# Two layers of a hybrid backbone with experts: outputs of six pairs by way of DRAM, inputs of layer 1 by gathers, shorter lists

## The chip, the cores and the metric

The kernel runs on one core of a Trainium2 chip (trn2). The metric is device time in microseconds (us); three runs of a kernel stand behind a median, and a trace of one profiled execution stands beside them.

## The reference

Two layers work on 256 latent and 256 context tokens of 1024 features, in float32. Each layer has a mixer (linear attention and grouped-query attention in layer 0, a state-space scan and a Fourier mix in layer 1) and then a mixture of 16 experts, of which each token uses two:

```python
idx, gates = route(tokens, router_w, router_b)      # two experts of one group of four
y = moe_ffn(tokens, idx, gates, exp_w_gate[layer], exp_w_up[layer], exp_w_down[layer])
x = layer_norm(alpha * x + m_lat[5] * y[n_ctx:].reshape(bsz, seq, d), ln_g[layer, 1], ln_b[layer, 1])
# an expert: (silu(xb @ w_gate) * (xb @ w_up)) @ w_down, hidden width 768
```

Layer 0 sends all 512 tokens through its experts, the last layer the 256 latent ones alone. The output is the latent stream.

## The kernel before

An expert's weights are six loads of 1.5 MB: four of gate and up (`in_egu`), two of down (`in_ed`). SyncE's queue (SP) issues them in order into slots (`wload`, L329); a load waits until PE has used what lay in its slot. Layer 0 has ten slots, layer 1 twelve.

The experts (`experts`, L1448) go two at a time, a pair. `route` gives every token its position in the lists of its two experts. `lists` (L1474) turns positions into a one-hot matrix G and, by a product with a table `aux` of four columns per token, into the slots' token numbers and gates. A list is cut into parts of 32 slots; S is the half (slots 0 to 63 or 64 to 127) of which a part is.

In layer 0 the tokens' rows lie in DRAM (`store`, L1431), and GpSimd (POOL) gathers those of a half list into the tile `xg` by an indirect DMA (`gather`, L1522); eight transposes per half bring features to the partitions (`features`, L1533, product `xt`). In layer 1 the rows stay in SBUF and the transposes are products with the one-hot matrix, two per block of features:

```python
for j in range(nb):
    self.mm(p[k // 4][:, (k % 4) * 128:(k % 4 + 1) * 128], xg[j][:, k * 128:(k + 1) * 128], G[S][:, j],
```

`hidden` (L1588) makes gate and up of each part (product `gu`), `down` (L1630) the outputs (product `dp`) of the expert before, whose results ACT and DVE take out of PSUM as a high and a low part `y`. `combine` (L1564) adds a pair's outputs to the tokens: DVE makes eight one-hot matrices, and PE multiplies them with `y`, 16 products of 512 columns in layer 0 (256 in layer 1) for the first half and 16 more where a list of the pair has over 64 slots (product `cm`); DVE adds the sums to `acc` (L1562). It comes one pair late, after gate and up of the second expert of the next pair.

Parts that a list doesn't reach are skipped by a branch (`when`, L1456): PE then runs a product with zeros in their place, so that PSUM holds zeros. In layer 0 the first two parts always run, in layer 1 the first. Lists over 128 slots would go through a loop of further windows at the end; the inputs have none. In layer 0 the fuller lists of the eight pairs have 74, 37, 62, 109, 101, 54, 67 and 61 slots, in layer 1 40, 39, 35, 68, 39, 38, 19 and 38 (worked out from the inputs with the reference's routing).

While the experts run, the order of PE's instructions is that of the program (`keep_in_program_order`); the other engines are ordered by a scheduler, and each engine works its list in order.

Of the kernel before, what the change touches and what calls it, by code (L numbers as in the profile page):

```python
# [8 lines left out]
F32 = mybir.dt.float32  # L9
# [23 lines left out]
NONE = 1024.0  # L33
R1, R2, R3 = 3, 4, (3, 5)
# weight slots in the areas while the experts run
# [3 lines left out]
# ---------------------------------------------------------------- host layout  # L39
# [13 lines left out]
# parameters and constants: '' for the whole run, 'A' and 'B' for the mixers of the two layers  # L53
# [79 lines left out]
def host_layout(a):  # L133
# [41 lines left out]
    # (layer, third, k, half, p, 1024): sixteen units per third, in loads of three and one  # L175
# [19 lines left out]
    # (l, e, k quarter, p, k, tile, gate or up, feature): each tile holds a quarter of the features  # L195
# [3 lines left out]
    # (l, e, half, p, b, output): the partitions hold the b-th 32 features of each quarter  # L199
# [56 lines left out]
# generators, each a step at a time  # L256
# [6 lines left out]
# pieces of one tile  # L263
# [11 lines left out]
class Core:  # L275
# [26 lines left out]
    # the four 16 KB areas b, o, a, x hold whatever lives across the parts of a layer  # L302
# [11 lines left out]
    # activations: a table set asked for is loaded behind those that need the one before, and before those that need it  # L314
# [62 lines left out]
    # between the layers: LayerNorm, and the modulated input of layer 1  # L377
# [29 lines left out]
    # out = x * exp(-ln(1 + exp(-x))); t is scratch  # L407
# [6 lines left out]
    # a third of layer l's adaLN rows for both streams, as per-partition scalars mods[l][:, m, kt, stream]  # L414
# [28 lines left out]

    def layer0(self):
# [27 lines left out]
    # acc = alpha * x + m2 * (o @ w_o); LayerNorm; v = modulated x for the experts; acc = alpha * x  # L472
# [31 lines left out]
    # layer 1's acc = alpha * x + m2 * (o @ w_o), over the features A of o, there before the others, and then B;  # L504
    # of the first N outputs all of A first
# [71 lines left out]
    # out = modulated, and x = alpha * (affine) of the normalized x, the stream h of acc  # L577
# [17 lines left out]
    # rows 0, 1: scale and offset of modulate(n * g + b); rows 2, 3: those of alpha * (n * g + b)  # L595
# [11 lines left out]
    # x (128, KT, n) <- (x - mean) / sqrt(var + eps) over the features, in place  # L607
# [32 lines left out]
    # a stream's LayerNorm, in parts of n tokens, each followed by what is done with it  # L640
# [18 lines left out]
    # scratch of normalize  # L659
# [9 lines left out]
    # x (in place) and its two parts, exact in float32r, of the modulated input  # L669
# [15 lines left out]
    # a weight chunk in two parts  # L685
# [8 lines left out]
    # x in two parts, exact in float32r  # L694
# [9 lines left out]
    # a product of two operands in parts: all but that of the two low parts, which is below float32's accuracy  # L704
# [7 lines left out]
    def even_mixer(self, uT, u, W):  # L712
# [6 lines left out]
        # low-rank decay inputs: partial sums over k on four column tiles  # L719
# [41 lines left out]
        # scratch: the places of the gated linear attention's later results, and the input's  # L761
# [35 lines left out]
    def attention(self, oT, gk, gv):  # L797
        nc, pt = self.nc, self.pt
        # the keys in two parts: the high one of each kv head on both halves of the partitions, the low one where the keys are
        kh = [pt.tile([128, T], F32R, name=f'kh{c}') for c in range(2)]  # L800
        kl = pt.tile([128, T], F32R, name='kl')
        for c in range(2):
            r = slice(c * 64, c * 64 + 64)
            for z in range(2):
                self.act(kh[c][z * 64:z * 64 + 64], gk[r], AF.Copy)
            nc.vector.tensor_tensor(kl[r], gk[r], kh[c][r].bitcast(F32), op=OP.subtract)
        for strm in range(2):
# [44 lines left out]
    def gla_states(self, i, q, k_, v, dec, mem):  # L852
# [3 lines left out]
        for di in range(2):  # L856
# [17 lines left out]
            # att[(cp, m), pair, l] = sum_d ke[d, m] qe[d, l], then its causal half  # L874
# [35 lines left out]
    def gla_heads(self, i, S, v, oT, mem):  # L910
        nc = self.nc
        for hh in range(2):
# [14 lines left out]
            # RMS norm over the value features  # L927
# [20 lines left out]
    # heads i (partitions 0-63, kv 0) and i + 4 (partitions 64-127, kv 1)  # L948
    def attend(self, q, k, v, oT, i, strm):
# [4 lines left out]
        # a head's queries in two parts, the high one where they are, the low one on the other half of the partitions  # L954
# [41 lines left out]
    # ------------------------------------------------------------ layer 1 mixer  # L996
# [21 lines left out]
    def odd_mixer(self, uT, parts):  # L1018
# [3 lines left out]
        # by streams: of the context's, nothing is needed once the states are there  # L1022
# [7 lines left out]
        # dt rows: heads of direction 0 at partitions 0-11, of direction 1 at 32-43  # L1030
# [19 lines left out]
        with tc.tile_pool(name='mixB1', bufs=1) as p1:  # L1050
# [17 lines left out]
            # token-major x and b, where the input was  # L1068
# [26 lines left out]
    def dt_tables(self, lr):  # L1095
# [28 lines left out]
        # weights of the tokens in their chunk's final state: dt * exp(sum of the later log decays)  # L1124
# [12 lines left out]
        # decay over the first latent chunk of each direction, on every partition  # L1137
# [38 lines left out]
    def ssd_heads(self, xb, xt, cs, HS, tabs, zs, oT, middle, last):  # L1176
# [4 lines left out]
        # the decays in two parts, exact in float32r, and what picks the rows of both  # L1181
# [266 lines left out]
    def experts(self, l, nb, pm, rows, xg, zero, pos, number, aux):  # L1448
# [25 lines left out]
        def lists(nm, n, e0, pos, aux, then=None):  # L1474
# [16 lines left out]
            if l:  # L1491
                if then:
                    then(Gs)
# [273 lines left out]
```

## Time and profile before

| | |
|---|---|
| median of three runs | 1545.85 us (1538.41 to 1550.7) |
| profiled execution, span from first to last instruction | 1528.9 us |
| PE busy | 1298.6 us, 85% |
| VectorE (DVE) busy | 755.5 us, 49% |
| mean DMA rate | 260 GB/s, 397.60 MB |

The profiled execution gives its span; the times of the runs also hold what lies around it, 16.95 us at the median. Layer 0's experts lie between about 389 and 860 us, layer 1's between about 1098 and 1507 us.

### The profile page before, as it was taken

What the parts mean: (1) busy time and instruction counts of PE and PEld (TensorE: products, weight loads), DVE (VectorE), ACT (ScalarE), POOL (GpSimd) and SP (SyncE); (2) the same over time, 40 slices, a digit from 0 to 9 for tenths busy, and PEclk for the clock granted to TensorE, in tenths of its full rate; (3) what the DMA queues carried; (4) which work ended last, traced back from release to release, by engine and by line L of the source; (5) the groups of instructions that cost most, each with busy time, mean ns of one, the idle gap of its engine ahead of it and who ended that gap; (6) DMA issues with size and microseconds to landing.
All of it is one profiled execution on the core that took longest, in us unless ns stands there. A gap on an engine that the chain in (4) does not pass through costs nothing. (4 is left out here: it accounts for less than half of the span.)

```text
span 1528.9 us, 28267 instructions
## 1 busy us (share of the span) xinstructions
PE 1298.6 (85%) x11753; PEld 799.5 (52%) x11754; DVE 755.5 (49%) x1899; ACT 417.4 (27%) x831; POOL 66.1 (4%) x68
## 2 busy tenths in 40 slices
PE   3999987996889889999988779989696778987774
PEld 0787643684334454665445348858442455544433
DVE  2756447776426233233344487567541544344534
ACT  3533243452112111111111243444321211121213
POOL 0000002011000000000000030030100000000000
PEclk8999988998899999999999989999898999999876
DMA  9322666044678978779987222652788998999931
GB/s 388 121 93 83 247 249 262 0 172 173 271 304 339 398 300 332 321 293 383 387 359 293 111 85 83 223 204 100 313 321 342 378 373 354 387 375 416 410 129 30
DMA packets 43700, 397.60 MB, mean 260 GB/s; under 512 B 4976, under 2 KB 9200, under 8 KB 12272
## 3 DMA queue, kind: packets, MB, share of 16 engines
q1 hardware_dynamic: 41200, 388.40, 63.1%
q0 software_dynamic: 1728, 4.20, 0.8%
q8 instruction: 158, 2.59, 0.7%
q10 hardware_dynamic: 576, 2.10, 0.3%
q14 instruction: 38, 0.31, 0.1%
HBM read 393.63 MB, written 3.15 MB: 260 GB/s over the span
## 5 line engine op out<-in xcount | busy, mean ns | idle before, releaser
L1599 DVE SCALAR_TENSOR_TENSOR h0p<-gu0p,gt0p,sg0p 128x192 f32<-128x192 f32 x64 | 25.1, 414 | 156.3 <-ACT sg0p L316 155.8
L1599 DVE SCALAR_TENSOR_TENSOR h1p<-gu1p,gt1p,sg1p 128x192 f32<-128x192 f32 x64 | 26.5, 414 | 142.2 <-ACT sg1p L316 142.2
L340 PE MATMUL gu1p<-more,big 128*32 128x384 f32 x976 | 87.2, 497 | 8.9 <-issue 5.1
L340 PE MATMUL gu0p<-big,xe0p 128*32 128x384 f32 x992 | 92.5, 494 | 0.2 <-DVE h0p L1599 0.2
L316 ACT ACTIVATE sg0p<-gu0p 128x192 f32<-128x192 f32 x64 | 19.7, 332 | 215.0 <-PE gu0p L340 211.8
L316 ACT ACTIVATE y0p<-dp0p 64x512 fp32r<-64x512 f32 x64 | 37.9, 591 | 147.9 <-PE dp0p L340 105.0
L340 PE MATMUL gu0p<-ring,xe0p 128*32 128x384 f32 x768 | 75.1, 490 | 1.5 <-ACT sg0p L316 0.8
L340 PE MATMUL gu0p<-more,xe0p 128*32 128x384 f32 x800 | 73.7, 488 | 0.9 <-issue 0.9
L1655 DVE TENSOR_TENSOR y0p<-dp0p,y0p 64x512 fp32r<-64x512 f32 x64 | 44.0, 688 | 58.2 <-ACT y0p L316 57.6
L340 PE MATMUL ada<-ring,small 128*32 128x512 f32 x344 | 60.1, 641 | 14.4 <-DMA ring<-in_ada 14.4
L316 ACT ACTIVATE sg1p<-gu1p 128x192 f32<-128x192 f32 x64 | 21.2, 330 | 183.5 <-PE gu1p L340 159.9
L340 PE MATMUL dp0p<-big,hT0p 128*32 128x256 f32 x792 | 59.6, 390 | 8.7 <-issue 6.1
L340 PEld LDWEIGHTS gu1p<-more,big 128*32 128x32 f32 x976 | 39.5, 112 | 51.6 <-issue 37.8
L1655 DVE TENSOR_TENSOR y1p<-dp1p,y1p 64x512 fp32r<-64x512 f32 x64 | 44.0, 688 | 42.9 <-ACT y1p L316 40.2
L340 PEld LDWEIGHTS gu0p<-big,xe0p 128*32 128x32 f32 x992 | 47.9, 111 | 32.9 <-issue 20.3
L316 ACT ACTIVATE y1p<-dp1p 64x512 fp32r<-64x512 f32 x64 | 37.8, 591 | 93.0 <-PE dp1p L340 49.1
L1562 DVE SCALAR_TENSOR_TENSOR big<-cm0p,mods,big 128x256 f32<-128x256 f32 x128 | 51.6, 476 | 20.0 <-PEq L1460 10.0
L340 PE MATMUL gu1p<-big 128*32 128x384 f32 x528 | 54.5, 521 | 4.0 <-issue 4.0
L340 PE MATMUL cm0p<-oh0p,y0p 128*128 128x512 f32 x192 | 55.2, 417 | 2.7 <-DVE big L1562 1.2
L316 ACT ACTIVATE big<-big 128x512 f32<-128x512 f32 (+2 forms) x81 | 44.7, 575 | 46.7 <-DVE big L626 19.4
L340 PE MATMUL zo<-zo,zw 128*128 128x256 f32 x384 | 54.6, 292 | 0.0
L340 PEld LDWEIGHTS zo<-zo,zw 128*128 128x128 f32 x384 | 48.6, 191 | 6.6 <-issue 4.3
(537 smaller groups left out, 2483.8 us busy)
## 6 DMA issues: line engine op xcount, KB each, us to landing
more<-in_egu SPq DMA_DIRECT2D x54, 1536.0 KB, 11.1
big<-in_egu SPq DMA_DIRECT2D x48, 1536.0 KB, 13.9
ring<-in_ada SPq DMA_DIRECT2D x27, 1536.0 KB, 7.3
ring<-in_ed SPq DMA_DIRECT2D x27, 1536.0 KB, 9.4
ring<-in_egu SPq DMA_DIRECT2D x26, 1536.0 KB, 10.1
big<-in_ed SPq DMA_DIRECT2D x21, 1536.0 KB, 10.6
more<-in_ed SPq DMA_DIRECT2D x16, 1536.0 KB, 10.6
ring<-in_odw SPq DMA_DIRECT2D x5, 1536.0 KB, 7.5
```

Of the source, the lines that this page charges most:

```text
L316: a = self.nc.scalar.activation(out, x, func, **kw)
L340: i = self.nc.tensor.matmul(out, lhsT, rhs, start=start, stop=stop, skip_group_check=True)
L1562: nc.vector.scalar_tensor_tensor(self.acc[:, h, f], y, self.mods[l][:, 5, f, h:h + 1], self.acc[:, h, f], op0=OP.mult, op1=OP.add)
L1599: nc.vector.scalar_tensor_tensor(H[:, t], p[:, 192:384], gt[:, 2 * m + t % 2, i, t // 2:t // 2 + 1], sg, op0=OP.mult, op1=OP.mult)
L1655: nc.vector.tensor_tensor(yl[r], dp[r], yh[r].bitcast(F32), op=OP.subtract)
```

## The change

Layer 0, pairs 0 to 5 (`NS = 6`): an output row is no longer added by one-hot products. The outputs are kept whole (one tile in place of a high and a low part), and four indirect DMAs per half list write them, 256 features each, to four planes in DRAM, at row token + 512 times the expert's rank (0 or 1) among the token's two. A fifth column of `aux` carries that row number. The planes are set to zero during the attention. After pair 5, GpSimd reads back the two rows of each token, 256 tokens at a time (16 DMAs of 128 rows of 1 KB, then two additions); PE transposes the sums (32 transposes in all), and DVE adds them to `acc`. Pairs 6 and 7 keep `combine`.

Layer 1: rows go to DRAM too, and pairs 1 to 7 gather them as layer 0 does; pair 0 keeps the one-hot products. Lists are made one pair earlier. Windows have 96 slots, so the fourth part (slots 96 to 127), its branches and zero products are gone, except the zeros for `dp`.

The one-hots of `combine` and the rows read back share one buffer `rb`.

```diff
+    def open_planes(self, pool):
+        z = pool.tile([128, 256], F32, name='zeros')
+        nc.gpsimd.memset(z, 0.0)
+        self.planes = [self.dram.tile([2 * T, 256], F32, name=f'plane{q}') for q in range(4)]
+        for p in self.planes:
+            nc.gpsimd.dma_start(p.rearrange('(a p) d -> p a d', p=128), z.unsqueeze(1).broadcast_to([128, 8, 256]))
...
+        if l == 0:
+            rk = top.rearrange('p (b g) j -> p b g j', b=nb)
...
+            nc.vector.tensor_scalar(rk, rk, 1.0 * T, -1.0 - NONE, op0=OP.mult, op1=OP.add)
+            nc.vector.tensor_tensor(aw[:, :, :, :, 4], rk, aw[:, :, :, :, 0].bitcast(F32), op=OP.add)
...
-        if l == 0:
-            nc.scalar.dma_start(self.rows[j * 128:(j + 1) * 128], x)
+        nc.scalar.dma_start(self.rows[j * 128:(j + 1) * 128], x)
...
+        def scatter(Y, to, i, e):
+            def send(S):
+                for q in range(4):
+                    nc.gpsimd.indirect_dma_start(out=self.planes[q], out_offset=bass.IndirectOffsetOnAxis(ap=to[:, q, i, S:S + 1], axis=0),
+                                                 in_=Y[S][:, q // 2, (q % 2) * 256:(q % 2) * 256 + 256].bitcast(F32), in_offset=None,
+                                                 bounds_check=2 * tn - 1, oob_is_err=False)
+            send(0)
+            n = nc.gpsimd.value_load(cnt[0:1, e:e + 1], min_val=0, max_val=T)
+            with tc.If(n > 64):
+                send(1)
+        def fetch(a):
+            rb = pm.tile([128, 2, 2, D], F32, tag='rb', name=f'rows{a}')
+            for j in range(2):
+                for i in range(2):
+                    for q in range(4):
+                        o = i * T + a * TC + j * 128
+                        nc.gpsimd.dma_start(rb[:, j, i, q * 256:(q + 1) * 256], self.planes[q][o:o + 128])
+            for j in range(2):
+                nc.gpsimd.tensor_tensor(rb[:, j, 0], rb[:, j, 0], rb[:, j, 1], op=OP.add)
+            return rb[:, :, 0]
+        def collect(got, a):
+            for c in range(KT // 2):
+                p = self.ps(f'cl{l}{a}{c}', 'b')
+                for k in range(2 * c, 2 * c + 2):
+                    for j in range(2):
+                        o = (k % 2) * TC + j * 128
+                        self.tr(p[:, o:o + 128], got[:, j, k * 128:(k + 1) * 128])
+                for k in range(2 * c, 2 * c + 2):
+                    add(k, a, p[:, (k % 2) * TC:(k % 2 + 1) * TC])
...
-                        if l:
+                        if G:
...
-            for t in (2, 3):
+            for t in range(2, nt):
                 swiglu(t, part(t))
...
-                    when(rv, 96, lambda: d_mm(1), lambda: z_mm(dp, 512))
+                    if nt > 3:
+                        when(rv, 96, lambda: d_mm(1), lambda: z_mm(dp, 512))
+                    else:
+                        z_mm(dp, 512)
...
             if m == 0 and e:
-                pend = (f'p{p - 1}', Y, *was)
+                if p > ns:
+                    pend = (f'p{p - 1}', Y, *was[:3])
+                else:
+                    scatter([y[0] for y in Y], *was[3:])
+                    if p == ns:
+                        got = fetch(0)
+            if ns and 1 <= e - 2 * ns <= 2:
+                collect(got, e - 2 * ns - 1)
+                if e == 2 * ns + 1:
+                    got = fetch(1)
```

Three places show how the order moves. The first is PE in layer 0, in expert 13, where the sum of pair 5 stood; `cm0p500` is its first PSUM tile, `gu0p613` the fourth part of expert 13, `xt0p710` the transposes for pair 7. Before:

```order
L340 MATMUL gu0p611_7427<-big_63,xe0p60_6965 32x384 x3
L340 MATMUL cm0p500_7517<-oh0p500_7501,y0p5000_6994 128x512
L340 MATMUL cm0p500_7517<-oh0p500_7501,y0p5001_6995 128x512
L340 MATMUL cm0p501_7518<-oh0p500_7501,y0p5000_6994 128x512
L340 MATMUL cm0p501_7518<-oh0p500_7501,y0p5001_6995 128x512
L1460 COMPARE_AND_BRANCH
L340 MATMUL gu0p613_7613<-ring_64,xe0p61_6978 32x384 x8
L340 MATMUL gu0p613_7613<-big_63,xe0p61_6978 32x384 x24
L1460 UNCONDITIONAL_BRANCH
L340 LDWEIGHTS zero0_2766
L340 MATMUL gu0p613_7613<-zero0_2766 128x384
L1460 UNCONDITIONAL_BRANCH
```

and now:

```order
L345 MATMUL gu0p611_7235<-big_63,xe0p60_6734 32x384 x3
L1487 COMPARE_AND_BRANCH
L345 MATMUL gu0p613_7347<-ring_64,xe0p61_6747 32x384 x8
L345 MATMUL gu0p613_7347<-big_63,xe0p61_6747 32x384 x24
L1487 UNCONDITIONAL_BRANCH
L345 LDWEIGHTS zero0_2776
L345 MATMUL gu0p613_7347<-zero0_2776 128x384
L1487 UNCONDITIONAL_BRANCH
L1487 COMPARE_AND_BRANCH
L350 MATMUL xt0p710_7408<-const_67,xg01_2062 128x128 x4
L350 MATMUL xt0p711_7409<-const_67,xg01_2062 128x128 x4
```

The products of the sum are gone, the part's branch follows the gate and up products directly, and the transposes for pair 7 come next. The second place is GpSimd behind layer 0's last gather. `xg01` is the second half's tile; `plane0` to `plane3` are the planes, `y0p500` and `y0p510` the outputs of pair 5 by half, `rows0` the first read back. Before:

```order
L1530 DMA xg00_2051<-rows_2053,idx0p2_3591 128x1024
L1460 UNCONDITIONAL_BRANCH x4
L1527 COMPARE_AND_BRANCH
L1530 DMA xg01_2052<-rows_2053,idx0p2_3591 128x1024
L1527 UNCONDITIONAL_BRANCH
L1527 ISA
L1527 UNCONDITIONAL_BRANCH
L1460 UNCONDITIONAL_BRANCH x28
L1730 TENSOR_LOAD cnt0_2899
```

and now, behind the scatters of pair 5 to planes 2, 3 and 0:

```order
L1598 DMA plane1_1412<-y0p500_6763,to0p2_3615 1024x256
L1603 COMPARE_AND_BRANCH
L1598 DMA plane0_1411<-y0p510_6764,to0p2_3615 1024x256
L1598 DMA plane1_1412<-y0p510_6764,to0p2_3615 1024x256
L1598 DMA plane2_1413<-y0p510_6764,to0p2_3615 1024x256
L1598 DMA plane3_1414<-y0p510_6764,to0p2_3615 1024x256
L1603 UNCONDITIONAL_BRANCH
L1603 ISA
L1603 UNCONDITIONAL_BRANCH
L1613 DMA rows0_7200<-plane0_1411 128x256
L1613 DMA rows0_7200<-plane1_1412 128x256
L1613 DMA rows0_7200<-plane2_1413 128x256
```

Where nothing stood before, GpSimd now has the scatters (those of the second half behind a branch) and then the 16 reads, in one queue. The third place is PE at the end of expert 12's down products (`dp0p600`), ahead of gate and up of expert 14 (`gu0p700`). Before:

```order
L340 MATMUL dp0p600_7697<-more03_2050,hT0p60_7460 32x256 x11
L340 MATMUL dp0p600_7697<-ring_64,hT0p60_7460 32x256 x12
L340 MATMUL dp0p600_7697<-more03_2050,hT0p60_7460 32x256 x12
L340 MATMUL gu0p700_7830<-more03_2050,xe0p70_7660 32x384 x8
L340 MATMUL gu0p701_7831<-more03_2050,xe0p70_7660 32x384 x8
```

and now:

```order
L345 MATMUL dp0p600_7427<-ring_64,hT0p60_7268 32x256 x12
L345 MATMUL dp0p600_7427<-more03_2060,hT0p60_7268 32x256 x12
L350 MATMUL cl000_7536<-const_67,rows0_7200 128x128 x4
L350 MATMUL cl001_7543<-const_67,rows0_7200 128x128 x4
L350 MATMUL cl002_7550<-const_67,rows0_7200 128x128 x4
L345 MATMUL gu0p700_7607<-more03_2060,xe0p70_7394 32x384 x7
L350 MATMUL cl003_7557<-const_67,rows0_7200 128x128 x4
L345 MATMUL gu0p700_7607<-more03_2060,xe0p70_7394 32x384
```

Four groups of four transposes (`cl000` to `cl003`) stand ahead of expert 14's first products.

## Rows read from the trace of the kernel before

**Rows 1.** The page: busy time by engine, and slices of 38.2 us in tenths

```profile
PE 1298.6 (85%) x11753; PEld 799.5 (52%) x11754; DVE 755.5 (49%) x1899; ACT 417.4 (27%) x831; POOL 66.1 (4%) x68
PE   3999987996889889999988779989696778987774
DMA  9322666044678978779987222652788998999931
```

**Rows 2.** Windows: us, busy us (instructions) by engine, clock, DMA share, GB/s

```profile
460.00:820.00 360.00, 337.09 (x3993) 194.03 (x3986) 136.28 (x309) 59.63 (x132) 9.00 (x9) 1.00 0.85 345
1100.00:1180.00 80.00, 64.14 (x641) 30.45 (x644) 27.15 (x115) 14.65 (x29) 0.00 (x0) 0.92 0.79 326
1180.00:1470.00 290.00, 231.57 (x2580) 135.69 (x2576) 127.64 (x442) 57.70 (x120) 0.00 (x0) 0.93 0.91 372
```

**Rows 3.** Waits of PE, 1180 to 1470 us: us in total, times, longest

```profile
PE gu1p L340 <- issue: 18.8, 6, 5.0
PE dp1p L340 <- issue: 13.3, 7, 2.8
PE dp1p L340 <- PEq L1460: 11.9, 5, 5.3
```

**Rows 4.** Timeline of PE in layer 1's experts: start, us, instruction, idle before

```profile
1203.67 0.50 PE L340 MATMUL gu1p<-zero 128*128 128x384 bf16 x2
1208.38 0.50 PE L340 MATMUL gu1p<-zero 128*128 128x384 bf16 x1 [4.21 <-issue]
```

**Rows 5.** DMA queues, 1180 to 1470 us: packets, MB, share of 16 engines

```profile
q8 instruction: 49, 0.80, 1.0%
```

**Rows 6.** Windows of PE, sum over the six stretches with layer 0's sums

```profile
sum 51.90, PE 45.86; mean PE 7.64
```

**Rows 7.** The same stretches, instructions of the one-hot sums (cm0p) alone

```profile
sum 51.90, PE 41.17 PEld 24.75 DVE 26.65; mean PE 6.86 PEld 4.13 DVE 4.44
```

**Rows 8.** Lines: count | busy us, mean ns | idle us before, releasers

```profile
L340 PE MATMUL xt1p<-small,xg 128*128 128x128 f32 x288 | 41.7, 293 | 7.6 <-ACT big L316 4.1 <-DVE hTr L1357 1.0 <-PEq L1460 0.9
L340 PE MATMUL gu1p<-zero 128*128 128x384 bf16 x38 | 12.1, 350 | 20.8 <-issue 15.7 <-DVE big L1562 3.1 <-DVE h1p L1599 0.9
L316 ACT ACTIVATE y0p<-dp0p 64x512 fp32r<-64x512 f32 x64 | 37.9, 591 | 147.9 <-PE dp0p L340 105.0 <-PEq L1460 42.5
L1562 DVE SCALAR_TENSOR_TENSOR big<-cm0p,mods,big 128x256 f32<-128x256 f32 x128 | 51.6, 476 | 20.0 <-PEq L1460 10.0 <-PE cm0p L340 10.0
L1204 POOL TENSOR_TENSOR big<-big,tab 128x768 f32<-128x768 f32 x2 | 3.9, 1926 | 0.1
```

**Rows 9.** Timeline of PE: eight transposes of a half list in layer 0

```profile
718.62 1.03 PE L345 MATMUL xt0p<-const,xg 128*128 128x128 f32 x8
```

**Rows 10.** Timeline of PE: down products that end pairs 5 and 6

```profile
749.42 1.67 PE L340 MATMUL dp0p<-ring,hT0p 128*32 128x256 f32 x23
...
782.58 0.42 PE L340 MATMUL dp0p<-more,hT0p 128*32 128x256 f32 x3
...
805.30 0.42 PE L340 MATMUL dp0p<-big,hT0p 128*32 128x256 f32 x3
```

**Rows 11.** Timeline of GpSimd (POOL): layer 0's first two gathers

```profile
384.54 1.20 POOL L1530 DMA_INDIRECT xg<-rows,idx0p  x1 [12.97 <-DVE tg0p L1510]
386.05 0.99 POOL L1530 DMA_INDIRECT xg<-rows,idx0p  x1 [0.31 <-issue]
```

**Rows 12.** Tile idx0p: the gathers' issue in ns, and their landing

```profile
L1530 POOL DMA_INDIRECT xg<-rows,idx0p x12: 985/990/1198, 384.5 to 706.0; - x12
DMA to landing us min/median/max: 3.6/9.3/13.7
```

**Rows 13.** DMA queues, 460 to 820 us

```profile
q0 software_dynamic: 1296, 3.34, 2.5%
```

**Rows 14.** Windows: one pair of layer 1's experts each

```profile
1183.40:1231.00 47.60, 38.08 (x453) 23.73 (x449) 21.37 (x74) 9.64 (x20) 0.00 (x0) 0.96 0.92 373
1330.00:1381.00 51.00, 45.31 (x533) 25.36 (x522) 21.37 (x74) 9.62 (x20) 0.00 (x0) 0.97 0.93 382
```

More of the change, by code (lines that the diff above doesn't have):

```diff
@@ L33 @@
 NONE = 1024.0
+NAUX = 5, 4
+WIN = 128, 96
+NS = 6
 R1, R2, R3 = 3, 4, (3, 5)
@@ L1388, in counts @@
         nc.vector.tensor_scalar(wf[:, 0], cf[:, NE:NE + NP], 0.0, None, op0=OP.is_gt)
-        for w in (128.0, 256.0, 384.0):
-            nc.vector.tensor_scalar(wf[:, 1], cf[:, NE:NE + NP], w, None, op0=OP.is_gt)
+        for w in range(WIN[l], T >> l, WIN[l]):
+            nc.vector.tensor_scalar(wf[:, 1], cf[:, NE:NE + NP], float(w), None, op0=OP.is_gt)
             nc.vector.tensor_tensor(wf[:, 0], wf[:, 0], wf[:, 1], op=OP.add)
@@ L1451, in experts @@
         NP = NE // 2
+        nt = WIN[l] // 32
         def z_mm(p, n):
@@ L1663, in experts @@
         info = {}
+        ns = 0 if l else NS
         def some_lists(b, n, then=None):
-            li = lists(f'p{b}', n, 2 * b, pos, aux, then)
+            li = lists(f'p{b}', n, 2 * b, pos, aux, then, max(0, b + n - ns) if n > 1 else int(b >= ns))
             for i in range(n):
@@ L1697, in between @@
                 if e == 0:
-                    features('p0', idx, full, xe, (1,))
-                    if l == 0:
-                        some_lists(1, 1)
-                        gathers(1)
+                    features('p0', full, xe, (1,), G0)
+                    some_lists(1, 1)
+                    gathers(1)
                 if m == 1 and pend:
@@ L1709, in experts @@
             if m == 1 and p + 1 < NP:
-                if l:
-                    some_lists(p + 1, 1)
-                nxt = features(f'p{p + 1}', info[p + 1][0][0], count(NE + p + 1), [])
+                if l and p + 2 < NP:
+                    some_lists(p + 2, 1)
+                nxt = features(f'p{p + 1}', count(NE + p + 1), [])
             if m == 1:
-                Y = outputs(f'p{p}')
+                Y = outputs(f'p{p}', 1 + (p >= ns))
             if last:
                 down(*last[:3], Wd, last[3], Y)
+            pend = None
             if m == 0 and e:
-                pend = (f'p{p - 1}', Y, *was)
-            last, was = [f'p{p}{m}', m, (f'p{p}{m}', H), rv], (tok, i, full)
+                if p > ns:
[8 more added lines that the diff above has]
+                    got = fetch(1)
+            last, was = [f'p{p}{m}', m, (f'p{p}{m}', H), rv], (tok, ti, full, to, i, NE + p)
             if e == 1 and l == 0:
@@ L1722, in experts @@
         down(*last[:2], transposed(*last[2]), load_d(NE - 1), rv, Y)
-        combine(f'p{NP - 1}', Y, tok, i, full)
+        combine(f'p{NP - 1}', Y, tok, ti, full)
         self.pin = False
@@ L1730, in experts @@
         most = nc.values_load(cnt[0:1, NE + NP:NE + NP + 1], min_val=0, max_val=T)
-        with tc.If(most > 128):
+        with tc.If(most > WIN[l]):
             pw = pm.tile([128, nb, 2], F32, name=f'pw{l}')
-            aw = pm.tile([128, nb, 2, 4], F32 if l else F32R, name=f'aw{l}')
+            aw = pm.tile([128, nb, 2, NAUX[l]], F32 if l else F32R, name=f'aw{l}')
             with tc.For_i(0, NE, 2) as e:
@@ L1738, in experts @@
                 with tc.For_i(1, n):
-                    nc.vector.tensor_scalar(pw, pw, -128.0, None, op0=OP.add)
-                    idx, tok, gt = lists('w', 1, 0, pw, aw)
+                    nc.vector.tensor_scalar(pw, pw, -1.0 * WIN[l], None, op0=OP.add)
+                    idx, tok, gt, _ = lists('w', 1, 0, pw, aw, tail=1)
                     for S in range(2):
                         gather(idx, 0, S)
-                    xe = features('w', idx, None, [])
-                    Y = outputs('w')
+                    xe = features('w', None, [])
+                    Y = outputs('w', 2)
                     for m in range(2):
```

120 lines of the change are left out of this document (68 added, 52 removed).

## The prediction

> **What bounds the kernel now.** I read the page first, then windows by stage, then what the tensor engine (PE) waits for, then the order of the instructions. The page [rows 1] gives PE 85% of the span, and its slices show two long stretches with the 16 DMA engines near full: those are the two expert stages. The windows [rows 2] tell them apart. In the middle of layer 0's experts (460 to 820 us) PE is busy for 337.09 of 360 us and the DMA engines for 0.85: PE is the limit, with 23 us to spare and the transfers 54 us behind it. In layer 1's experts (1180 to 1470) PE is busy for 231.57 of 290, the DMA engines for 0.91. There the transfers of weights are the nearer limit, and PE has idle time on its own path: the waits [rows 3] give 18.8 + 13.3 + 11.9 us of "issue" and sequencer time. In the timeline [rows 4] such a gap stands between two zero products, 4.21 us long, with no operand to wait for. The instruction queue [rows 5] moved 49 blocks of 16 KB in the 290 us, on the same DMA engines as the weights; I take the gaps for PE waiting for its code.
>
> The Trainium skill (Runtime: NRT & Kernel Launch, section "Instruction fetch mechanics") says that a branch to code outside the loaded blocks stops the engine until a DMA has brought the block. By that rule fewer branches and less code shorten layer 1's PE path; the gap next to a skipped block agrees. No term below is taken from the rule.
>
> **Layer 0, what goes.** The weighted one-hot sums of six of eight pairs. The lists of pairs 0, 3 and 4 go over 64 slots (worked out from the inputs), so they cost 32 products each, the other three 16: 144 of 192. The six stretches in which they stand (481.8 to 492.4 the first, 768.6 to 776.4 the last) take 51.9 us in all; PE is busy there for 45.9 us [rows 6], with the sums alone for 41.2 [rows 7], so 6.0 us are waits. I count 41.2 and half of the 6.0: -44. The one-hots, the low halves of the outputs and the adds that go with them are on VectorE, which is busy for 136.28 of the 360 us [rows 2]: nothing.
>
> **Layer 0, what comes on PE.** 32 transposes, at 1.03 us for eight [rows 9]: +4. Six small operations in the routing and a few in the lists, on the path to the first gather: +1. The new tables of row numbers take the place of the old ones.
>
> **Layer 0, the way back from DRAM.** This is the term that decides. The order puts the transposes of the first half straight behind the down products of expert 12, and they wait for the rows; everything behind them on PE waits too, the gate and up products of expert 14 first. In the timeline [rows 10] the last down product of pair 5 starts in the block at 749.42 and ends at 751.1, and the place of the new transposes is at 782.6 to 783: 31.4 us, less the sum of pair 5 that is gone (a sixth of the 44, with its 16 products 6.2): 25.2 us. In that time must go: a copy out of PSUM (1 us, above the 0.591 of such a piece [rows 8]), four scatters on GpSimd's queue, each at the 0.99 us of a gather and the 0.31 between two [rows 11]: 5.2; their landing; 16 reads; their landing; the last addition of 128x1024. A read is not in this trace. Its issue costs between 0.5 and 1.3 us (half a gather, and one with its gap); I take 1.15, 18.4 in all. Landing is 3.6 to 13.7 us, median 9.3, for the gathers [rows 12]; 9.3 while weights flow and 5 once PE stands still. An addition is 1.9 us at 768 columns [rows 8], so 2.5 at 1024. Sum 1 + 5.2 + 9.3 + 18.4 + 6.5 + 2.5 = 42.9 (6.5 between 5 and 9.3), less 25.2: a wait of 18. For the second half 18.4 + 9 + 2.5 = 29.9 stand against the about 20 us from the first transposes to the second place at 805.3 [rows 10]: 10. Together +28. Bounds: 0 if issue and landing are at their low ends (1 + 2.5 + 3.6 + 8 + 3.6 + 2.5 = 21, under 25.2), 45 at the high ones (1 + 5.2 + 13.7 + 20.8 + 9.3 + 2.5 = 52.5, so 27, and 18 for the second).
>
> The Trainium skill (DMA: Bandwidth & Descriptors, section "Anatomy of one DMA — SWDGE (gpsimd) path") gives about 2.0 us and the bytes over 436 GB/s for one such DMA, 2.3 us for these 128 KB (an estimate). The shortest landing, 3.6 us for 512 KB, agrees; the median of 9.3 beside the weights does not. With 2.3 in place of each landing the waits would be about 10 and the time 18 us less; I keep the measured median.
>
> **Layer 0, bytes.** About 806 rows of 4 KB are written and 1024 read, 7.5 MB. Gathers moved 3.34 MB in 2.5% of 360 us, 9 us [rows 13], 2.7 us per MB: +20 us of all DMA engines (rows of 1 KB may cost more; none is in the trace). The engines had 306 of 360 us of work, so 326 now: the stage can't come under that, a gain of 34 at most. Busier engines bring PE's code later: layer 1, at 0.91, loses 44 us in 290 to such gaps. Between 0 and +20, I take +4. Setting the planes to zero (4 MB) falls into the attention, where slices read 0 to 4 tenths of DMA [rows 1]: nothing; without that cover about 11 us.
>
> Layer 0: -44 + 4 + 1 + 28 + 4 = -7.
>
> **Layer 1.** Gathered rows need 8 transposes per half list in place of 16 products in two passes each. The 288 records (two to a product) are nine half lists, 41.7 us [rows 8], 4.6 each; pair 0 stays as it is. Eight change: 8 x (4.6 - 1.03) = 29. The fourth part is taken by no list here (the longest has 68); its 16 zero products are 16 of the 38 with 12.1 us and 20.8 of waits before them [rows 8]: 14. A quarter less code (528 to 398 products per pair in the order): of the other gaps about 8. So PE's path is some 50 us shorter, and the transfers set the end: idle DMA time is 26 us in 1180 to 1470 and 17 in 1100 to 1180 [rows 2]. The gathers bring 2 MB, 5 us; the stores fall before the weights' rush. At most 38 can go; the first pair's 12 or so of idle DMA stay, since that pair waits for routing. I take -26, bounds -5 and -38. The gathers are issued a pair ahead (47.6 to 51 us [rows 14] against 13.7 at worst [rows 12]), so nothing waits for them. The tail behind the last weights hardly changes.
>
> **Sum.** 1528.9 - 7 - 26 = 1495.9 for the profiled span. The median of the runs is 16.95 us above that span; with the same distance 1512.9, 1513. A measurement of this kernel tells about 1% from no change, 1530.4 to 1561.3.
>
> **Rivals.**
> (a) The rows are back in time. The low end of landing (3.6) speaks for it, the median against. Then layer 0 gives its most, 34, and layer 1 its 26: 1486.
> (b) Layer 1 is bound by weights alone, and PE's gaps only move. For it: a DMA share of 0.91 and a full 20 us here and there; against it: the engines' idle time. Layer 1 gives 5, the sum is -12: 1534, no change.
> (c) Slower: GpSimd's queue becomes the path at layer 0's end. Reads of 1 KB rows queue between weight packets, the waits reach 45, PE's code comes 20 us later, and layer 1's gaps grow with its gathers so that it gives 8: -44 + 4 + 1 + 45 + 20 - 8 = +18: 1564. It decides as soon as waits and late code in layer 0 exceed 39 us and what layer 1 gives.
> (d) VectorE holds up the descriptors of GpSimd's DMAs. The twelve gathers took 985 to 1198 ns to issue [rows 12] with VectorE busy for 38% of the stretch, so the trace shows nothing of it. If each of 36 issues waited for half an addition of VectorE (0.476 us [rows 8]), the waits would be 8 us more: 1521.
> The Trainium skill (SBUF — State Buffer, under "Who interferes with whom") states (d) as a rule: a two-port VectorE operation locks GpSimd out, and descriptors wait. It speaks against this change, which puts 16 reads where VectorE copies.
>
> **Chances.** My case 0.44, (a) 0.24, (b) 0.17, (c) 0.09, (d) 0.06. Below 1530.4 lie nearly all of mine, (a) and most of (d): faster 0.70. Same 0.21, mostly (b). Slower 0.09. The range goes from beyond (a), with layer 1 at -34, to beyond (b): 1478 to 1550.
>
> **What would show it.** In the profile after: no one-hot sums for pairs 0 to 5, and layer 0's pairs 6 to 8 us shorter each; a wait of 15 to 20 us before the first collecting transposes and about 10 before the second; layer 1's pairs at 44 to 46 us from 47.6 to 51 [rows 14] with a DMA share near 0.97. I am wrong if the collecting transposes do not wait, if layer 0's pairs do not shrink, or if layer 1 keeps its length though PE's products are gone.

## The result, and the profile after

The changed kernel takes 1478.57 us (median of four runs, 1474.16 to 1480.49); the kernel before, beside it, 1546.52 (1538.41 to 1550.7). The recorded ratio is 0.958, with an interval from 0.955 to 0.961 (the two medians alone give 0.956). The forecast was 1513 us, so the gain was twice the one forecast and the time just inside the low end of the range, 1478.

The page of the kernel after, against [rows 1]: busy time by engine, the slices (36.9 us each now), and the instruction queue's row.

```profile
PE 1250.3 (85%) x11433; PEld 726.9 (49%) x11434; DVE 682.2 (46%) x1773; ACT 398.0 (27%) x791; POOL 140.8 (10%) x153
...
PE   4999988898679799999878867998978688898774
...
DMA  9421688134488998889998341273388999999981
...
q8 instruction: 140, 2.29, 0.6%
```

PE's share of the span is the same 85%. What changed is the end of the DMA row: layer 1's experts now have seven slices of 9 running, where [rows 1] has 8, 8, 9, 9, 8 and four of 9.

The windows of the kernel after (us, busy us of PE, PEld, DVE, ACT, POOL, granted clock, DMA share, GB/s). The first is layer 0's stage, from its first gate and up product to its last one-hot sum; the second its middle, as in [rows 2]; then layer 1's stage in three pieces (1437 us is where the last weights land), and two of its pairs.

```profile
393.20:849.80 456.60, 405.23 (x4774) 196.03 (x4774) 110.88 (x289) 60.12 (x136) 72.47 (x82) 0.96 0.86 348
...
460.00:820.00 360.00, 321.14 (x3909) 157.72 (x3898) 77.15 (x192) 46.55 (x110) 71.48 (x81) 0.96 0.91 371
1100.60:1175.00 74.40, 58.44 (x636) 26.09 (x635) 31.18 (x155) 12.58 (x26) 2.12 (x2) 0.91 0.84 349
1175.00:1437.00 262.00, 219.32 (x2440) 109.85 (x2438) 120.24 (x408) 54.72 (x110) 5.94 (x6) 0.91 0.99 415
1437.00:1453.80 16.80, 13.13 (x163) 8.08 (x162) 10.96 (x24) 6.02 (x9) 0.00 (x0) 0.87 0.04 14
1182.10:1226.90 44.80, 38.41 (x431) 19.36 (x430) 22.46 (x88) 8.62 (x18) 1.98 (x3) 0.89 0.99 414
1272.20:1317.60 45.40, 42.51 (x503) 21.94 (x503) 20.42 (x74) 9.10 (x18) 0.99 (x1) 0.93 1.01 425
```

The same pieces of the kernel before: layer 0's stage, and layer 1's up to its last weights and behind them.

```profile
391.10:856.20 465.10, 428.82 (x4886) 235.95 (x4886) 176.51 (x419) 74.46 (x160) 9.99 (x10) 0.98 0.80 325
1104.80:1180.00 75.20, 59.34 (x607) 25.64 (x611) 26.29 (x111) 13.45 (x27) 0.00 (x0) 0.93 0.82 337
1180.00:1469.00 289.00, 230.57 (x2565) 135.26 (x2560) 126.66 (x441) 57.70 (x120) 0.00 (x0) 0.93 0.91 373
1469.00:1505.50 36.50, 27.76 (x281) 15.13 (x273) 16.03 (x35) 7.34 (x13) 0.00 (x0) 0.81 0.02 4
```

The span fell by 51.5 us, from 1528.9 to 1477.4. Layer 0's stage starts 2.1 us later and is 8.5 shorter (465.1 to 456.6). The mixer between the layers is some 2 us longer. Layer 1's stage is 47.5 shorter: 400.7 before, 353.2 now. Up to the last weights it is held by its transfers now, at a share of 0.99 and 415 GB/s.

PE's waits from 1175 to 1437 us in the kernel after, against [rows 3], and the instruction queue there, against [rows 5]:

```profile
PE gu1p L345 <- issue: 12.1, 5, 5.4
...
PE dp1p L345 <- issue: 3.6, 3, 2.0
...
PE gu1p L345 <- PEq L1487: 2.9, 8, 0.7
```

```profile
q8 instruction: 35, 0.57, 0.8%
```

"Issue" and sequencer time, 44.0 us in [rows 3], is 18.6 in these three rows, and 35 blocks of code arrived instead of 49.

These windows leave out the start of the stage, where the changed kernel's longest "issue" gap stands, and that one isn't code. PE's timeline, and what its sequencer did in the gap:

```profile
1153.10 2.79 PE L345 MATMUL dp1p<-big,hT1p 128*32 128x256 f32 x24 [9.51 <-issue]
...
L1737 PEldq TENSOR_LOAD <-cnt x14: 298/302/312, 1143.0 to 1152.0; - x14
```

PE reads 14 list lengths there, one behind the other, 0.30 us each and 0.68 us from one to the next. The kernel before reads six in the same place, in a gap of 4.75 us.

The way back from DRAM in layer 0: GpSimd's timeline from the last scatter of pair 5 to the second half's last addition, and PE's at the two places where it collects (start, us, instruction, idle before).

```profile
737.69 0.98 POOL L1598 DMA_INDIRECT plane<-y0p,to0p  x1 [0.30 <-issue]
744.22 0.62 POOL L1613 DMA_DIRECT2D rows<-plane  x1 [5.55 <-DMA plane<-y0p,to0p]
745.78 3.73 POOL L1613 DMA_DIRECT2D rows<-plane  x7 [0.93 <-DMA plane<-y0p,to0p]
750.46 4.22 POOL L1613 DMA_DIRECT2D rows<-plane  x8 [0.95 <-DMA rows<-plane]
754.70 2.38 POOL L1615 TENSOR_TENSOR rows<-rows 128x1024 f32<-128x1024 f32 x1
766.62 2.34 POOL L1615 TENSOR_TENSOR rows<-rows 128x1024 f32<-128x1024 f32 x1 [9.54 <-issue]
...
796.51 2.34 POOL L1615 TENSOR_TENSOR rows<-rows 128x1024 f32<-128x1024 f32 x1 [8.82 <-issue]
```

```profile
769.01 2.61 PE L350 MATMUL cl<-const,rows 128*128 128x128 f32 x11 [8.21 <-POOL rows L1615]
...
798.90 3.46 PE L350 MATMUL cl<-const,rows 128*128 128x128 f32 x15 [4.76 <-POOL rows L1615]
```

PE waits 8.2 and 4.8 us for the rows. The 9.54 us ahead of the second addition have "issue" beside them; I read them as the landing of the reads, since that addition needs the last ones.

### The profile page after: what moved, and what is told of

The parts are those of the page before. It is cut to its first block, busy times and chain, and to the rows that moved or that the text cites. A ratio compares the mean times of both kernels' runs of the same rounds, so it can differ in the third digit from the quotient of the medians.

```text
span 1477.4 us, 27647 instructions
## 1 busy us (share of the span) xinstructions
PE 1250.3 (85%) x11433; PEld 726.9 (49%) x11434; DVE 682.2 (46%) x1773; ACT 398.0 (27%) x791; POOL 140.8 (10%) x153
## 5 line engine op out<-in xcount | busy, mean ns | idle before, releaser
L1665 DVE SCALAR_TENSOR_TENSOR h1p<-gu1p,gt1p,sg1p 128x192 f32<-128x192 f32 x48 | 19.9, 415 | 118.0 <-ACT sg1p L321 117.9
L345 PEld LDWEIGHTS gu1p<-more,big 128*32 128x32 f32 x976 | 35.1, 111 | 51.3 <-issue 46.1
L345 PEld LDWEIGHTS gu0p<-big,xe0p 128*32 128x32 f32 x992 | 37.8, 111 | 45.4 <-issue 42.1
L321 ACT ACTIVATE y0p<-dp0p 64x512 f32<-64x512 f32 (+1 forms) x40 | 23.6, 591 | 132.9 <-PE dp0p L345 105.0
L321 ACT ACTIVATE sg1p<-gu1p 128x192 f32<-128x192 f32 x48 | 15.9, 330 | 156.4 <-PE gu1p L345 141.0
L1598 POOL DMA_INDIRECT plane<-y0p,to0p x36 | 35.6, 988 | 205.8 <-ACT y0p L321 180.0
L345 PE MATMUL zo<-zo,zw 128*128 128x256 f32 x384 | 54.7, 292 | 0.0
L345 PE MATMUL dp0p<-ring,hT0p 128*32 128x256 f32 x624 | 48.9, 401 | 3.5 <-issue 3.2
L345 PEld LDWEIGHTS <-zero 128*128 128x128 bf16 x105 | 10.0, 97 | 83.2 <-issue 64.8
```

Source lines behind the costliest of these rows:

```text
L321: a = self.nc.scalar.activation(out, x, func, **kw)
L345: i = self.nc.tensor.matmul(out, lhsT, rhs, start=start, stop=stop, skip_group_check=True)
L1598: nc.gpsimd.indirect_dma_start(out=self.planes[q], out_offset=bass.IndirectOffsetOnAxis(ap=to[:, q, i, S:S + 1], axis=0), in_=Y[S][:, q // ...
L1665: nc.vector.scalar_tensor_tensor(H[:, t], p[:, 192:384], gt[:, 2 * m + t % 2, i, t // 2:t // 2 + 1], sg, op0=OP.mult, op1=OP.mult)
```

## The experiments

e1 to e7 and e9 stand in one table with the changed kernel and the one before (its time is the median of the runs beside them, 1540.0 to 1540.4; the changed kernel's ratio is to the 1546.5 beside it). "Stops" is PE's idle time in layer 1's stage that the waits put down to issue or PE's sequencer; runs of list lengths are in it, about 8 us before, 7 in e4, 12 in e6 and after. "Code" is the instruction queue's blocks there. "1.2 GHz" is the time at a granted clock of 0.50, from the clock of pieces of 10 us each.

| | time, us | ratio to before | layer 0 | layer 1 | stops | code | 1.2 GHz in layer 1 |
|---|---|---|---|---|---|---|---|
| before (profile) | 1540 | | 465.1 | 400.4 | 62 | 65 | 65 |
| e5 tiles alone | 1541.4 | 1.002 (1.000 to 1.004) | 466.4 | 404.5 | 58 | 65 | 66 |
| e1 layer 0 alone | 1544.3 | 1.002 (0.999 to 1.006) | 458.4 | 414.6 | 67 | 65 | 76 |
| e9 layer 0 alone, padded | 1544.2 | 1.003 (1.001 to 1.005) | 450.6 | 417.3 | 62 | 66 | 89 |
| e4 layer 0 and gathers | 1533.7 | 0.994 (0.991 to 0.997) | 454.4 | 408.1 | 59 | 63 | 103 |
| e7 changed, with dead code | 1523.1 | 0.989 (0.984 to 0.994) | 451.3 | 400.4 | 48 | 63 | 89 |
| e2 layer 1 alone | 1498.0 | 0.972 (0.967 to 0.977) | 471.9 | 360.3 | 35 | 48 | 69 |
| e3 layer 0 and short lists | 1483.0 | 0.962 (0.957 to 0.967) | 461.3 | 350.5 | 26 | 51 | 29 |
| e6 fourth part as zeros | 1480.9 | 0.961 (0.956 to 0.966) | 453.9 | 351.5 | 32 | 48 | 46 |
| after | 1478.6 | 0.958 (0.955 to 0.961) | 456.6 | 352.8 | 32 | 48 | 65 |

**Which layer, which part.** The first four kernels take the change apart: layer 0's part alone, layer 1's alone, and with layer 0's part each half of layer 1's. (In the kernels with lists of 128 slots, three small tables of layer 1 lie elsewhere, to make room.)

```diff
 e1  -WIN = 128, 96
     +WIN = 128, 128
...
     -                nxt = features(f'p{p + 1}', count(NE + p + 1), [])
     +                nxt = features(f'p{p + 1}', count(NE + p + 1), [], G=G0)
...
 e2  -NS = 6
     +NS = 0
...
 e3  -                nxt = features(f'p{p + 1}', count(NE + p + 1), [])
     +                nxt = features(f'p{p + 1}', count(NE + p + 1), [], G=G0)
...
 e4  -WIN = 128, 96
     +WIN = 128, 128
```

> Layer 0 as changed; layer 1 as before (one-hot inputs, windows of 128). Theory A (layer 0's gain was eaten by two waits, 8.2 + 4.8 us, and by some 31 us at the lower clock that follow them; the large gain lies in layer 1): layer 0's stage, from its first gate and up product to its last sum, 457 us as in the changed kernel (465.5 before), layer 1's 398 to 402 (400.7 before, 353.2 changed); time 6 to 12 us under the kernel before. Rival B (layer 1 gained from layer 0's change too, by where the weights' slots and the code stand when it begins): layer 1 under 390 us, time 20 us or more under before.

> Layer 1 as changed; layer 0 with its one-hot sums for all eight pairs. Theory A: layer 0 464 to 467 us, layer 1 351 to 356, time 45 to 50 us under the kernel before plus whatever of the 16 us between the profile of before and its median belongs to layer 1. Rival B: layer 1 at 365 us or more.

> Layer 0 as changed; in layer 1 the lists of 96 slots alone, inputs by one-hot products for every pair. Theory A (PE's path was the limit, and its parts add until the transfers are the limit at full rate): the fourth part's zero products and gaps and a part of the code go, 14 + 8 us: layer 1 375 to 382 us, DMA share 0.93 to 0.96. Rival C (either part alone brings the stage to the transfers' limit): layer 1 353 to 360. Rival D (the gaps only move, the products of the inputs are all that counts): 392 or more.

> Layer 0 as changed; in layer 1 gathered inputs alone, lists of 128 slots with their fourth part. Theory A: eight half lists cost 3.6 us less each on PE, 29 us: layer 1 369 to 375 us, DMA share 0.95 to 0.98. Rival C (either part alone reaches the transfers' limit): 353 to 360. Rival D (only the inputs' products count): also 353 to 360, with the lists alone at 392 or more.

Short lists alone bring layer 1 to 350.5 us and the time to 1483.0, 61 us under e1. Gathers alone bring 408.1 and 1533.7, 11 us under e1. My split, 29 us for the gathers and 22 for the lists, had the sizes the wrong way round, and theory A, which rested on it, falls. Rival C is nearest for the lists alone (353 to 360 us). e4's 408.1 us is over every range given for it (353 to 360 and 369 to 375). Of the first two kernels, e1's 414.6 us lies over both of its ranges (398 to 402, and under 390), and e2's 360.3 between its two (351 to 356, and 365 or more). In e4, too, PE's busy time in the stage is less (313.0 us from 327.1 in e1), but more of it runs at 1.2 GHz, 103 us from 76. e1 gains nothing over before although its layer 0 is shorter: its layer 1 is 10 us longer than in e5.

**What the fourth part cost.** No list here reaches it, so its products never run. Two kernels tell its work from its code. e6 has lists of 128 slots and keeps the fourth part's zero products and what ACT and DVE do with them, but has no branch and no product for it. e7 is the changed kernel, with branches and products added that never run.

```diff
 e6  +                if l and t == 3:
     +                    z_mm(p, 384)
     +                    return p
...
     -                    if nt > 3:
     +                    if l == 0:
                             when(rv, 96, lambda: d_mm(1), lambda: z_mm(dp, 512))
...
 e7  +            if l and rv is not None:
     +                p4 = self.ps(f'gu{l}{nm}3', 'pj' if m else 'b')
     +                when(rv, 96, lambda: [gu_mm(2, jj, p4) for jj in range(4)])
...
     +                            when(rv, 96, lambda: d_mm(0))
```

> The changed kernel with lists of 128 slots in layer 1, but of their fourth part only the zero products, ACT's and VectorE's work on them; its branches and its products, which no list here ever ran, are not in the program (so lists over 96 would lose those slots). Theory G (the time was in loading PE's code, of which the fourth part is a quarter though it never runs): layer 1 353 to 362 us as with short lists, 43 to 47 instruction packets between its first and last gate and up products. Rival H (the time was in the fourth part's work itself): layer 1 390 us or more as with the gathers alone (408).

> The changed kernel with code added in layer 1 that never runs: behind each expert's gate and up products and inside its down products one branch on lists over 96 slots, with as many products as the fourth part had. Theory G: layer 1 395 to 410 us, 56 to 61 instruction packets, issue gaps of PE as with the gathers alone (50 us and more); time 1520 to 1535. Rival H: layer 1 353 to 360 us, time 1478 to 1486.

Layer 1's stage in the windows of e4, e6 and e7, in this order (columns as above), and the instruction queue's row of e4 and e6:

```profile
1100.40:1508.80 408.40, 313.00 (x3252) 158.38 (x3252) 171.45 (x602) 78.24 (x160) 8.07 (x8) 0.87 0.81 331
```

```profile
1104.00:1455.50 351.50, 291.05 (x3252) 142.13 (x3251) 170.40 (x602) 78.14 (x160) 8.05 (x8) 0.94 0.92 384
```

```profile
1095.60:1496.00 400.40, 303.85 (x3235) 154.62 (x3235) 161.60 (x586) 73.61 (x144) 8.05 (x8) 0.89 0.83 338
```

```profile
q8 instruction: 63, 1.03, 1.0%
```

```profile
q8 instruction: 48, 0.79, 0.9%
```

e4 and e6 run the same 3252 matmuls, and the same 602 and 160 instructions on DVE and ACT. e6 is 57 us shorter. PE is busy for 22 us less, stops for 28 less and waits for operands 7 less (34.9 to 27.7 us). Most of the busy time is the clock: 58 us less at 1.2 GHz would give up to 29. e7 runs the changed kernel's 3235 matmuls and takes 48 us more in layer 1, 44 in all. Theory G holds on both sides: the time lay in code that was loaded or jumped over and never ran. Which of the two, loading or jumping, these kernels do not separate, since branches and blocks go together in both. From the first gate and up product to the last, as the forecasts had it, e6 takes 45 blocks and e7 58, both within their ranges. e7 also takes one more PSUM tile per expert; its waits for ACT and VectorE, 25.8 us against 28.5 in the changed kernel, are no longer for it.

e7's 48 us of stops show a part of the price only. Its waits put another 21 us down to DMA, as if PE had waited for weights. The two longest of these:

```profile
1157.79 2.79 PE L345 MATMUL dp1p<-big,hT1p 128*32 128x256 f32 x24 [9.54 <-DMA ring<-in_egu]
...
1211.08 2.79 PE L345 MATMUL gu1p<-big 128*32 128x384 f32 x16 [5.32 <-DMA ring<-in_ed]
```

In the first, PE's sequencer reads the 14 list lengths again. The second ends 1.5 us after a block of code has arrived (1208.6 to 1209.6 us), and so do, by 1.5 and 2.0 us, the other two (5.1 and 1.2 us). The same sign can be counted over all of PE's idle stretches of 1 us or more in layer 1, runs of list lengths aside: 22 of 28 in e7 end within 2.2 us after a block's arrival, half of them within about 1.5, and make 53.1 us together (50 and more were forecast; blocks come every 6 us there, so chance would give about a third). It is 22 of 30 and 54.7 us in e4, 21 of 23 and 51.8 us before, but 10 of 17 and 18.0 us in e6, and 7 of 13 and 18.2 us in the changed kernel. By this sign the stops for code differ by 35 us (e7 against the changed kernel) and by 37 (e4 against e6); most of what is left of the 48 and 57 us is PE's busy time, 13 and 22 us more.

**Does layer 0's change move layer 1's stops?** e1's layer 1 is longer than before's with the same code. e5 has the new tiles alone, with neither planes, gathers nor short lists; e9 adds to e1 a branch with 32 products that never run.

```diff
 e9  +            if l and e == 0:
     +                pp = self.ps('pad', 'b')
     +                when(rv, 400, lambda: [self.mm(pp[:, :128], self.C('ident'), self.C('ident')) for _ in range(32)])
```

> The kernel before with one part of the change only, the new layout of the tiles that hold an expert pair's outputs and the one buffer for its one-hots; no planes, no gathers in layer 1, lists of 128 slots. Layer 1 was 414.6 us long with layer 0's change alone and 400.4 in the profile of before. Theory E (layer 0's change as such moves where layer 1's stops fall): this one stays within 1% of the kernel before, layer 1 398 to 405 us. Rival F (the new tiles cost layer 1 the 14 us): layer 1 410 us or more, time 8 us or more over before.

> Layer 0 as changed, layer 1 as before, and ahead of layer 1's first expert one branch with 32 products of 128x128 that never run. Without them layer 1 took 414.6 us, with layer 0 as before and the same layer 1 404.5. Theory E (where code lies decides how often PE stops in layer 1, and layer 0's change moved it): layer 1's length differs by 8 us or more from 414.6, in either direction, with as many instruction packets (60). Rival J (layer 1 is longer behind the new layer 0 for another reason, its start or its transfers): 410 to 419 us, time within 5 us of 1544.

The tiles cost nothing (rival F falls). The pad moved the time by 0.1 us and layer 1 by 2.7, so where the code lies, as far as one such pad tells, is not the reason, and theory E falls. (That is no case against theory G: e7 added 32 skipped parts, and its 48 us are 1.5 for each.) Behind the new layer 0, an old layer 1 shows 10 to 24 us more at 1.2 GHz (e1 and e9 against e5), which would account for 5 to 12 of the 10 to 13 us. A new layer 1 is 7.5 us shorter behind it (e2 and after). So layer 0's change is worth 20 us of time with the new layer 1 (1498.0 to 1478.6) and nothing with the old one (1541.4 to 1544.3). Why layer 1 differs is open.

**Layer 0: the waits, and code again.** e8 collects later, e11 reads the rows a pair earlier (the first half's without pair 5), e10 makes the fourth part zeros in six pairs, as e6 did in layer 1, and e12 is the changed kernel once more beside e9 to e11.

```diff
 e8  +                if ns and e == 2 * ns + 2:
     +                    collect(got[0], 0)
     +                    got[0] = fetch(1)
...
     +                if ns and e == 2 * ns + 3:
     +                    collect(got[0], 1)
...
 e10 +                if t == 3 and nm[:2] in SHORT:
     +                    z_mm(p, 384)
     +                    return p
...
     -                    if nt > 3:
     +                    if nt > 3 and nm[:2] not in SHORT:
...
 e11 -                    if p == ns:
     +                    if p == ns - 1:
                             got = fetch(0)
...
     +            if ns and e in (2 * ns, 2 * ns + 2):
     +                collect(got, (e - 2 * ns) // 2)
```

> The changed kernel with the collecting transposes later: the first half's behind the first gate and up products of expert 14, the second half's amid those of expert 15; the same work. Theory A (the waits of 8.2 and 4.8 us, and the lower clock behind them, lie on the path): no wait of over 1 us before either, layer 0 457 to 438 to 446 us, time 1460 to 1470. Rival I (the transfers, at a share of 0.97 there, take the freed time): layer 0 452 us or more, time 1474 to 1480.

> The changed kernel with the fourth part of layer 0's lists made zeros without branches in the six pairs whose lists end before slot 96 (so longer lists there would lose slots); pairs 3 and 4 keep it. Layer 0 took 451 to 461 us in the seven kernels with the changed layer 0. Theory G (code that is skipped costs in layer 0 as well): 10 to 25 us less, layer 0 430 to 446 us, time 1454 to 1468. Rival I (layer 0 is held by its transfers and its own products): 450 us or more, time 1474 to 1484.

> The changed kernel with the rows read back one pair earlier and collected in experts 12 and 14, each two experts behind its read (the first half's rows so miss the outputs of pair 5); the same number of transfers and products. Theory A (the waits of 13 us and the lower clock behind them are on the path): no wait of over 1 us for the rows, layer 0 10 to 20 us shorter, 436 to 446 us, time 1458 to 1468. Rival I (the transfers hold layer 0's end anyway, as a later collecting had its wait again): 450 us or more, time 1472 to 1484.

> The changed kernel once more, beside the last three on the same chip: 1474 to 1484 us, layer 0 451 to 461 us, layer 1 350 to 354 us by every theory.

PE's waits for the rows, in layer 0's stage, of e8 and e11, and e10's window of the stage:

```profile
PE cl L350 <- POOL rows L1615: 16.8, 3, 11.9
```

```profile
PE cl L350 <- POOL rows L1615: 6.0, 1, 6.0
```

```profile
392.60:825.00 432.40, 389.07 (x4774) 188.65 (x4774) 110.19 (x289) 59.30 (x136) 72.50 (x82) 0.96 0.89 367
```

e8 takes 1482.7 us (1480.3 to 1483.6), no better than the changed kernel, and still waits 16.8 us: its second half's last addition starts 31 us after that half's first read, with the DMA engines at a share of 1.01 from 760 to 800 us. (That half's reads start behind the first half's collecting, so collecting later delayed them too.) e11 takes 1474.1 (1473.3 to 1475.8) against 1478.2 of e12 (1475.2 to 1484.8). Of the waits, 6.0 us are left of 13, but its time and its layer 0, 450.7 us, lie in rival I's ranges. The 4 us between the medians are no clear gain either: the changed kernel's fastest runs take 1474.2 and 1475.2 us, and its code of layer 0 took 450.6 to 461.3 us in eight profiles. So theory A is not borne out, and what the waits cost is not shown. Even two experts ahead, the reads took from 701.6 to 733.7 us to arrive among the weights; each of the last eight was issued only after one of the first eight had landed. e10 takes 1461.8 (1458.6 to 1464.6), 16 us less: layer 0 is 432.4 us long, its stops 7.5 us where the changed kernel has 24.2 and its blocks 50 where that has 60. It does so although its waits for rows grow to 25.2. So skipped code costs in layer 0 as well. (The stage is 24 us shorter and the time 16; its layer 1 is 5 us longer, 357.9, with the code of the changed kernel.) None of the three is a better kernel as it stands: e8 is no faster, e10 would lose slots 96 to 127 of a longer list in six pairs, though no list here has them, and e11 leaves pair 5 out of the first half's rows. e12's layer 0 takes 459.2 us and its layer 1 353.3.

## Why the prediction was right in sign and half the size

**The offset.** The median of before was taken as its span plus 16.95 us "around it". In all thirteen kernels that have both, the profiled run's time is 1.7 to 2.2 us above its span. The profiled execution of before was simply a short one: its 1528.9 us of span lie below every timed run of before (1533.0 is the shortest of 49). That step cost 15 of the 34 us by which 1513 was too high. It also means that the stages compared below explain the 51.5 us of the spans; where the other 16 of the medians' 68 us lie, no trace of before shows.

**The range.** That 1478.6 lies inside is luck. The low end was made of 34 us from layer 0 and 34 from layer 1, and neither came so: layer 0 gave 8.5, and layer 1's 47.5 is outside the bounds that it was given, 5 and 38.

**Layer 1: −26 forecast, −47.5 measured.** PE's path was to get 50 us shorter, which is near. The step that failed is the cap, "at most 38 can go". It counted the idle time of the DMA engines up to 1470 us and added that the tail behind the last weights hardly changes. From the first product to the last weights the stage lost 28 us (364.2 to 336.4), as forecast. Behind the last weights it lost 19.7 (36.5 to 16.8): PE had fallen behind its transfers by gaps such as the 4.99 us before a zero product at 1459.1, and ran the tail at a granted clock of 0.81, now 0.87. A tail behind the last transfer is time of the engine that lags, and shrinks with it.

The 50 were also split wrongly. The fourth part's zero products and gaps, and the code, stood in the sum at 14 + 8; short lists measured 61. The gathers stood at 29 and measured 11 alone. On top of short lists (e3 and after) the time is 4 to 5 us less, but layer 1's stage is not shorter (350.5 and 352.8 us), so that they gave layer 1 anything there is not shown. Eight half lists took 1.94 us each (15.5 us for 64 transposes) and not 1.03, since most came in pieces between other products and some at the lower clock. What I priced was the work of the fourth part; what counted was that each skipped part was in the program. The Trainium skill (Runtime: NRT & Kernel Launch, section "Instruction fetch mechanics") says that a taken branch out of the loaded blocks stops the engine until the target has come; e6 and e7 agree, with 15 blocks fewer and 57 us, and the other way 48. The prediction named the rule and took no term from it.

**Layer 0: −7 forecast, −8.5 measured, by errors that cancel.** The agreement is luck twice over: the new layer 0 took 450.6 to 461.3 us in eight profiles and the old one 465.1 to 471.9 in three, so one pair of profiles could have shown −4 or −21.
- Sums gone and transposes added: −44 + 4 = −40 expected. PE's busy time fell by 23.6 us. The transposes took 7.4 us. The granted clock of 460 to 820 us fell from 1.00 [rows 2] to 0.96. At 0.50, which is 1.2 GHz, PE ran 24 us more over the stage, up to 12 us of time. PE stood 8.2 and 4.8 us before two of these stretches and had stopped several times ahead of the others. The sum had no term for that.
- Waits for rows: +28 expected, 13.0 measured. The reads' issue was at fault: 0.54 us each and not 1.15, so 16 took 10.5 us and not 18.4. The scatters took 4.8 us and landed in 5.6 (5.2 and 9.3). The reads landed in 12 us after the last issue, where I had 6.5. Both errors of the landings stay within the 3.6 to 13.7 of [rows 12]. (The landing of 3.6 us, read in the prediction as one of 512 KB, was that of pair 0's ten rows over 64, 40 KB; the 128 rows of its first half took 4.6.)
- Later code: +4 expected, −0.9 measured (stops of 25.1 and 24.2 us). Planes: nothing, as said.
- The pairs shrank by 3 us each, not by 6 to 8: from the transposes for pair 2 to those for pair 7, five pairs, it was 265.0 us before and is 249.0.

**The rivals.** (a) came nearest with 1486, for another reason: the rows were not back in time, and layer 0 gave 8.5 us and not 34. (b) has fallen: layer 1 gave far more than 5. After the change, it is bound by weights, as (b) said of before. (c) has fallen. (d): the reads took 0.536 to 0.622 us to issue and the scatters 0.977 to 1.029, gathers before 0.985 to 1.198 [rows 12], so nothing shows that GpSimd's descriptors were held up; what the Trainium skill (SBUF — State Buffer, "Who interferes with whom") states of the lock does not show in these numbers.

**What would show it.** Pairs of 44.8 and 45.4 us at a DMA share of 0.99 and 1.01 in layer 1 were forecast (44 to 46, near 0.97); so was a wait at both collecting places, at half its size.

## What to carry to other kernels

Count code that is only ever skipped as a cost: on a kernel that branches around unused tiles, the number of instruction blocks per stage, and "issue" time next to skipped work, tell more than the zero products do. Look at what the sequencer does in such a gap, too: 12 of the changed kernel's 32 us in layer 1 were reads of list lengths. When a stage seems bound by transfers, look at what lies behind the last transfer before capping a gain by idle DMA time. And take the profiled execution's place among the timed runs from their spans, not from the median.

## What the runs showed of the hardware

- Products that never run, with the branches around them, cost layer 1 about 48 to 57 us (e7 against after, e4 against e6); 15 blocks of 16 KB of code went with them.
- PE's stops for code end about 1.5 us after a block has arrived, and the waits can put them down to a DMA into a tile that the product behind them does not read (5.32 us in e7).
- A list length read on PE costs 0.68 us; 14 in a row are a gap of 9.5 us that the waits call issue or DMA.
- Stops can cost more than their own length: between e4 and e6, 37 us of stops for code went together with 58 us at 1.2 GHz, between e7 and the changed kernel 35 with 24. It is no fixed price: e3 and the changed kernel, with 26 and 32 us of stops, ran 29 and 65 us there.
- A direct DMA is issued by GpSimd in 0.54 us, an indirect one in 0.98. Sixteen reads of 128 KB then landed 12 us after the last issue, among weights at a DMA share of 0.94 to 1.00 (740 to 780 us).
